# Hybrid mLSTM and stick-breaking layer on one core: each block of turned heads stored to DRAM by one transfer, regrouped by its four reads, and some of the moves at other places

## The chip, the cores and the metric

One core of a Trainium2 chip runs the whole layer in one launch. The metric is the device time of one execution in microseconds; lower is better. TensorE multiplies, VectorE (DVE), ScalarE (ACT) and GpSimd (POOL) do the rest, and SyncE (SP) issues nearly all transfers, one after the other.

## What is computed

One layer over x of 512 tokens by 1024 channels in float32, with one combined input projection whose columns feed two token mixers and the merge gates:

```python
h = rmsnorm(x, norm_w)
proj = h @ w_in + b_in
mq, mk, mv, mi, mf, mo, mz, sq, sk, sv, sz, gates = split(proj)

q, k = split(silu(causal_conv(concat(mq, mk))))          # mLSTM, 4 heads of 256
hm = mlstm_chunkwise(q, k, mv, mi, log_sigmoid(mf))
y_m = rmsnorm(hm) * sigmoid(mo) * silu(mz)

q, k = rmsnorm(sq), rmsnorm(sk)                          # stick-breaking, 8 heads of 128
z = q @ k.T * 128 ** -0.5                                # strictly causal
A[t, s] = sigmoid(z[t, s]) * prod(1 - sigmoid(z[t, j]) for s < j < t)
y_s = (A @ sv) * silu(sz)

g_m, g_s = split(sigmoid(gates))
out = x + (g_m * (y_m @ w_proj_m) + g_s * (y_s @ w_proj_s)) @ w_out
```

## The kernel before

Each float32 operand of a matmul is split into a high part (ACT copies it to float32r: `wh`) and a low part (DVE subtracts: `wl`), and a product is three matmuls (`mm3`, lines 96 to 98; line 966 in the `Half` units): high by high, high by low, low by high.

**Units.** The work of TensorE is a list of units, and the main loop (line 1500) runs over them. A unit has a weight slab of 512 KB: `load` issues it on SP into a tile `stg` (three buffers), `split` makes `wh` and `wl` (three buffers each) two units ahead, and `mm(0)` and `mm(1)` are its two halves. In the loop's body the order of the code is the order on each engine; the tables at the top of the file say in which unit the other work is written, and `defer(n, f)` writes `f` n units later. `E` is 36. The units before E are the first q group (4), four of a gate path, and two `Pair`s of 14 `Half` units of 12 matmuls each, which form products by a recursive scheme with sums of weight quarters (`X`, `Y`, `V`, `Z`) and of results (`dst`, to which GpSimd adds a tile `u` by an accumulating transfer). From E on most units have 24 matmuls. Unit E starts in the trace at 138.25 us.

**Turning q and k.** The stick-breaking heads need q and k with the channel on the partitions. For each of two sets of four heads, and for q and k, two heads (a pair g) are moved at a time:

- `turn` (in unit `TURN[name][g]`, for set 0): DVE transposes the 32x32 blocks of 256 channels by 512 tokens into a tile `ty` (line 437), four instructions.
- `move`, one unit later: SP stores `ty` to DRAM as `t_d`, four transfers of 32 partitions each (line 443).
- `back` (in unit `TZ_BACK[name, g]`, for set 0): SP reads it back, four transfers (line 450), into `tz`, where channels lie on partitions in the natural order. For q DVE then multiplies by the product of the two norm weights (line 453).
- `head(h)` starts at `SB_START`: it splits `tz` into `qtt` and `ktt` (lines 101 and 102), then scores, chains the products by a scan, and turns the result in the same way by `ay`, `a_d`, `az`.

Set 0's q is turned in units 9 and 13, so its store is long done when it is read back; its k comes out of the second `Pair` late, and is turned in units 30 and 31, with the first head starting in unit E-1. The mLSTM heads turn their output in the same way, by `ht`, `h_d` and `hz` (lines 865 to 897). The tiles `ty` of set 0, `tz`, `qtt`, `ktt`, the raw q and the `dst` pairs share nine buffers of the tag `qk`; which one a tile gets is settled when the program is built, by what is free at that place.

In units E-1 and E besides: `gates()` (line 611) runs 16 matmuls for the mLSTM gates, and ACT copies their result (line 621).

A transfer on SP also waits until the one eight places before it has landed, since eight completion semaphores are used in turn.

Of the kernel before, what the change touches and what calls it, by code (L numbers as in the profile page):

```python
# [8 lines left out]
F32 = mybir.dt.float32  # L9
# [3 lines left out]
OP = mybir.AluOpType  # L13

D = 1024
T = 512
KT = 8
TB = 4
# [10 lines left out]
E = 4 + FILL + 14 * PAIRS  # L29
SB_START = [E + n for n in (-1, 2, 5, 8, 14, 16, 18, 20)]  # L30
M_START = [E + n for n in (37, 41, 54, 60)]
GATES_PREP, GATES_START, GATES_SCAN = E - 3, E - 1, E + 26
TURN = {"q": (9, 13), "k": (30, 31)}
TZ_BACK = {("q", 0): E - 4, ("q", 1): E + 1, ("k", 0): E - 3, ("k", 1): E + 2}
REST = {E + n for n in (7, 48)}
AHEAD, LOADS = 2, 4

# [2 lines left out]
def tile_hybrid_layer(  # L40
# [16 lines left out]
    nc = tc.nc  # L57
# [3 lines left out]
    def pool(name, bufs=1, **k):  # L61
        return ctx.enter_context(tc.tile_pool(name=name, bufs=bufs, **k))
# [3 lines left out]
    sp = pool("sp")  # L66
    mp = pool("mp")
    tiny = pool("tiny", 4)
    dp = pool("dp", space=bass.MemoryType.DRAM)
# [9 lines left out]
    def blk(tag, dt=F32, shape=(512,), name=None, p=128):  # L79

        where = mp if tag in MISC else sp
        return where.tile([p] + list(shape), dt, name=name or tag, tag=tag, bufs=BUFS[tag])

    def two(tag, dt=F32, name=None):

        t = blk(tag, dt, (2, 512), name=name)
        return t[:, 0, :], t[:, 1, :]
# [12 lines left out]
    def split(src, hi, lo):  # L100
        nc.scalar.activation(hi, src, AF.Copy)  # L101
        nc.vector.tensor_tensor(lo, src, hi.bitcast(F32), op=OP.subtract)  # L102
# [96 lines left out]
    now = [0]  # L199

    def defer(n, fn):
        later.setdefault(now[0] + n, []).append(fn)
# [26 lines left out]
    qkw = cst.tile([128, 1], F32, name="qkw")  # L229
# [124 lines left out]
    class SbSet:  # L354
# [71 lines left out]
        def turns(self, name):  # L426
            for g in range(2):
                if self.s:
                    defer({"q": (1, 2), "k": (1, 2)}[name][g], lambda g=g: self.turn(name, g))
                else:  # L430
                    later.setdefault(TURN[name][g], []).append(lambda g=g: self.turn(name, g))

        def turn(self, name, g):
            ty = sp.tile([128, 8, TB, 32], F32, name="ty", tag=("qk", "A")[self.s],
                         bufs=BUFS[("qk", "A")[self.s]])
            for tb in range(TB):
                nc.vector.transpose(ty[:, :, tb, :],  # L437
                                    self.raw[name][tb][:, 256 * g:256 * g + 256].rearrange("p (x j) -> p x j", j=32))

            def move():  # L440
                park = dp.tile([32, 2, 4, 4, 128], F32, name="t_d", tag="t_d", bufs=4)
                for a in range(4):
                    nc.sync.dma_start(park[:, :, :, a].rearrange("i h b x -> i (h b) x"),  # L443
                                      ty[32 * a:32 * a + 32].rearrange("i g n j -> i g (n j)"))

                def back():
                    tz = blk("qk", F32, (2, 4, 128), name="tz")
                    self.tz[name, g] = tz
                    for b in range(4):
                        nc.sync.dma_start(tz[32 * b:32 * b + 32].rearrange("i h a x -> i h (a x)"),  # L450
                                          park[:, :, b].rearrange("i h a x -> i h (a x)"))
                    if name == "q":
                        defer(2, lambda: nc.vector.tensor_scalar(tz, tz, qkw, None, op0=OP.mult))

                if self.s:
                    defer(1, back)
                else:
                    later.setdefault(TZ_BACK[name, g], []).append(back)

            defer(1, move)  # L460
# [11 lines left out]
        def head(self, h):  # L472
            hs = slice(h * 128, (h + 1) * 128)
            tr = []
            for name in ("q", "k"):
                th, tl = own = two("qk", FR, name=name + "tt")
                tp = self.tz[name, h // 2][:, h % 2].rearrange("p a (i j) -> p i a j", j=32)
                th, tl = [x.rearrange("p (i a j) -> p i a j", a=4, j=32) for x in own]
                split(tp, th, tl)
                tr.append(own)  # L480
# [66 lines left out]
            park = dp.tile([4, 32, 4, 320], F32, name="a_d", tag="a_d", bufs=3)  # L547
# [11 lines left out]
            def turn(js):  # L559
# [5 lines left out]
                for j in js:  # L565
                    o, n = (slot[j, j] - n0) * 128, T - j * 128
                    a_parts[j] = ah[:, o:o + n], al[:, o:o + n]

            turn((0,))
            turn((1,))  # L570
            yield
            op = att_ps()
# [5 lines left out]
            apply(0)  # L578
            apply(1)
            turn((2, 3))  # L580
            yield
            apply(2)
# [117 lines left out]
    class MPair:  # L700
# [89 lines left out]
        def head(self, h):  # L790
# [48 lines left out]
            hns = blk("P5", shape=(TB, 256), name="hns")  # L839
# [22 lines left out]

            ht = sp.tile([128, 8, TB, 32], F32, name="ht", tag="A", bufs=4)

            def turn(i):
                nc.vector.transpose(ht[:, :, i, :], hns[:, i, :].rearrange("p (x j) -> p x j", j=32))

            scale = [num(0), num(1)]  # L870
            for i in (2, 3):
                yield
                for fn in scale:
                    fn()
                if i == 3:
                    turn(0)
                    turn(1)
                scale = [num(i)]
            yield
            scale[0]()  # L880
            turn(2)
            yield
            turn(3)
            yield
            hz = sp.tile([128, 2, T], F32, name="hz", tag="A", bufs=4)
            park = dp.tile([32, 2, 4, 4, 128], F32, name="h_d", tag="h_d", bufs=2)
            for b in range(4):
                nc.sync.dma_start(park[:, :, :, b].rearrange("i d a x -> i (d a) x"),
                                  ht[32 * b:32 * b + 32].rearrange("i g n j -> i g (n j)"))
            yield  # L890
            for a in range(4):
                nc.sync.dma_start(hz[32 * a:32 * a + 32], park[:, :, a].rearrange("i d b x -> i d (b x)"))
            yield
            for d in range(2):
                y = y_m[2 * hd + d].rearrange("p (i b j) -> p i b j", i=TB, b=4)
                z = hz[:, d, :].rearrange("p (b i j) -> p i b j", i=TB, b=4)
                nc.vector.tensor_tensor(y, z, y, op=OP.mult)


# [600 lines left out]
    for c in range(N):  # L1500
# [34 lines left out]
        for e in list(pend):  # L1535
            if c >= e[0] and e[2]():
                pend.remove(e)
                g = e[3]()
# [36 lines left out]
```

## Time and profile before

| | |
|---|---|
| time, median of 3 runs | 685.08 us (683.88 to 686.15) |
| the profiled execution | 685.25 us, its span 683.5 us, 9343 instructions |
| TensorE busy | 672.9 us, 98% of the span |
| DVE, ACT, POOL busy | 506.3, 366.5, 121.6 us |
| transfers | 116.70 MB, 133200 packets on SP's queue, 53.1% of 16 engines' span |

The page gives busy time by engine, the span in 40 slices, the DMA queues, the chain of work that ended last, and the costliest groups of instructions. Further views of the same trace list who waited for whom, the instructions of an engine in order of time, and the busy share, granted TensorE clock and DMA share of any stretch. Times in them are counted from the span's start. A wait in square brackets names how long the engine stood idle before an instruction and what released it. Where a row ends in x4, four instructions were merged.

### The profile page before, as it was taken

The page shows a single profiled execution, that of the slowest core. Times are in us where ns is not written, and L with a number is a line of the kernel's source. Part 1 is how long each engine was busy: PE and PEld are TensorE (multiplying, and loading weights), DVE is VectorE, ACT ScalarE, POOL GpSimd, SP SyncE. Part 2 cuts the span into 40 slices and gives each one's busy share as a digit, 9 for nine tenths or more (in the row PEclk, how much of TensorE's full clock was granted, in tenths as well). Part 3 has the DMA queues.
Part 4 walks back from the last instruction along what each step waited for, and adds up shares of the span by engine and source line. Part 5 has one row for each costly group of instructions (what it writes and reads, how often), then busy time and mean ns, then how long its engine had stood idle before and what let it go on. Part 6 is the DMA issues. An engine that isn't in the chain of part 4 may idle for free.

```text
span 683.5 us, 9343 instructions
## 1 busy us (share of the span) xinstructions
PE 672.9 (98%) x3098; PEld 560.8 (82%) x3098; DVE 506.3 (74%) x866; ACT 366.5 (54%) x696; POOL 121.6 (18%) x259
## 2 busy tenths in 40 slices
PE   8999999979999999999999999999999999999998
PEld 6888888858888888888888888888888888888876
DVE  6887988748788868978788654569973466477997
ACT  7576567244776365644654747344455854234451
POOL 4023153212545013310011101110000120001020
PEclk9999999999999999999999999999999999999999
DMA  7567785796758976737368632435344478957333
GB/s 251 144 209 191 223 210 119 165 306 209 210 158 234 270 213 194 215 117 207 93 129 184 140 107 62 133 100 153 93 139 126 124 222 258 275 183 161 116 82 103
DMA packets 137568, 116.70 MB, mean 171 GB/s; under 512 B 17658, under 2 KB 108180, under 8 KB 137520
## 3 DMA queue, kind: packets, MB, share of 16 engines
q1 hardware_dynamic: 133200, 106.02, 53.1%
q0 software_dynamic: 4176, 9.96, 8.0%
q8 instruction: 24, 0.39, 0.2%
q14 instruction: 24, 0.20, 0.1%
q10 hardware_dynamic: 144, 0.13, 0.1%
HBM read 85.10 MB, written 21.03 MB: 155 GB/s over the span
## 4 chain that ended last, share of the span: by engine, by line
PE 78%; DMA 2%; DVE 2%; SPq 1%; issue 1%; ACT 0%; ACTq 0%; DVEq 0%
PE dps L96 22%; PE dps L97 22%; PE dps L98 22%; PE aps L97 3%; PE aps L98 3%; PE aps L96 3%; DMA stg<-in_w_in_dram 1%; PE aps L848 1%; PE aps L850 1%; PE aps L849 1%; DMA dst<-u 1%; DVE wl L102 1%; SPq L450 0%; SPq L443 0%; DVE ty L437 0%
## 5 line engine op out<-in xcount | busy, mean ns | idle before, releaser
L96 PE MATMUL dps<-hh,wh 128*128 128x512 f32 x448 | 175.0, 391 | 0.0
L98 PE MATMUL dps<-hh,wl 128*128 128x512 f32 x448 | 174.6, 390 | 0.0
L97 PE MATMUL dps<-hl,wh 128*128 128x512 f32 x448 | 174.4, 389 | 0.0
L102 DVE TENSOR_TENSOR wl<-stg,wh 128x1024 fp32r<-128x1024 f32 x79 | 96.5, 1222 | 81.5 <-ACT wh L101 80.8
L101 ACT ACTIVATE wh<-stg 128x1024 fp32r<-128x1024 f32 x79 | 83.1, 1054 | 57.6 <-PE dps L97 27.4
L98 PEld LDWEIGHTS dps<-hh,wl 128*128 128x128 f32 x448 | 84.1, 188 | 17.8
L97 PEld LDWEIGHTS dps<-hl,wh 128*128 128x128 f32 x448 | 84.2, 188 | 16.7
L96 PEld LDWEIGHTS dps<-hh,wh 128*128 128x128 f32 x448 | 84.2, 188 | 16.7
L97 PE MATMUL dps<-wl,hh 128*128 128x512 f32 x96 | 37.8, 393 | 0.8 <-DVE wl L102 0.8
L738 ACT ACTIVATE tmp<-acc 128x512 f32<-128x512 f32 x16 | 10.1, 633 | 52.9 <-DVE acc L735 52.9
L96 PE MATMUL dps<-wh,hh 128*128 128x512 f32 x96 | 38.0, 396 | 0.0
L98 PE MATMUL dps<-wh,hl 128*128 128x512 f32 x96 | 37.6, 392 | 0.0
L735 DVE SCALAR_TENSOR_TENSOR acc<-tmp,vec,acc 128x511 f32<-128x511 f32 (+2 forms) x48 | 36.0, 750 | 1.7
L501 POOL TENSOR_SCALAR_AFFINE_SELECT om<-om 128x128 f32<-128x128 f32 x32 | 19.8, 617 | 90.4 <-ACT om L499 90.3
L499 ACT ACTIVATE om<-aps,rq 128x512 f32<-128x512 f32 (+3 forms) x32 | 16.8, 524 | 18.3 <-PE aps L98 18.3
L511 DVE TENSOR_TENSOR_SCAN om<-om 128x512 f32<-128x512 f32 (+3 forms) x32 | 26.2, 819 | 0.0
L96 PE MATMUL dps<-yh,wh 128*128 128x512 f32 x64 | 24.9, 389 | 0.0
L97 PE MATMUL dps<-yl,wh 128*128 128x512 f32 x64 | 24.9, 389 | 0.0
L98 PE MATMUL dps<-yh,wl 128*128 128x512 f32 x64 | 24.9, 389 | 0.0
L858 ACT ACTIVATE hns<-aps,hst 128x256 f32<-128x256 f32 x16 | 7.6, 475 | 27.8 <-DVE hst L857 20.8
L97 PEld LDWEIGHTS dps<-wl,hh 128*128 128x128 f32 x96 | 18.3, 191 | 4.5 <-DVE wl L102 1.1
L96 PEld LDWEIGHTS dps<-wh,hh 128*128 128x128 f32 x96 | 18.3, 191 | 3.7 <-ACT wh L101 0.2
(299 smaller groups left out, 1510.7 us busy)
## 6 DMA issues: line engine op xcount, KB each, us to landing
stg<-in_w_in_dram SPq DMA_DIRECT2D x71, 512.0 KB, 4.8
a_d<-ay SPq DMA_DIRECT2D x8, 640.0 KB, 2.9
az<-a_d SPq DMA_DIRECT2D x32, 160.0 KB, 5.4
t_d<-ty SPq DMA_DIRECT2D x32, 128.0 KB, 3.7
tz<-t_d SPq DMA_DIRECT2D x32, 128.0 KB, 4.5
stg<-in_w_proj_s_dram SPq DMA_DIRECT2D x8, 512.0 KB
B<-in_w_out_dram SPq DMA_DIRECT2D x8, 512.0 KB, 6.9
stg<-in_w_proj_m_dram SPq DMA_DIRECT2D x8, 512.0 KB, 3.6
```

Source lines behind the costliest of these rows:

```text
L96: nc.tensor.matmul(ps, ah, bh, start=first, stop=False)
L97: nc.tensor.matmul(ps, ah, bl, start=False, stop=False)
L98: nc.tensor.matmul(ps, al, bh, start=False, stop=last)
L101: nc.scalar.activation(hi, src, AF.Copy)
L102: nc.vector.tensor_tensor(lo, src, hi.bitcast(F32), op=OP.subtract)
L499: nc.scalar.activation(om[:, 0:n], zp, AF.Sigmoid, scale=rn[:, h:h + 1])
L501: nc.gpsimd.affine_select(out=om[:, ts], in_=om[:, ts], compare_op=OP.is_gt, fill=1.0, base=0, channel_multiplier=1, pattern=[[-1, 128]])
L511: nc.vector.tensor_tensor_scan(back, back, back, 1.0, op0=OP.mult, op1=OP.bypass)
L735: nc.vector.scalar_tensor_tensor(acc[:, j:], t[:, 0:T - j], cw(3 - j, ch), acc[:, j:], op0=OP.mult, op1=OP.add)
L738: nc.scalar.activation(t, acc, AF.Sigmoid)
L848: nc.tensor.matmul(nm[:, 0:258], ph, vh, start=j == 0, stop=False)
L858: nc.scalar.activation(hn, sum_v, AF.Square, scale=dn, accum_out=ssq)
```

## The change

The store of a turned block becomes one transfer of 128 whole rows of 4 KB, in the order in which `ty` (or `ht`) lies in memory; DVE's turns write `ty` in the order b, h, n, j, so that what one read needs from a row is one run of 256 floats. The four reads regroup: each takes a quarter of every row, 1 KB, in place of runs of 2 KB. `tz` and `hz` then hold (4, 256) per partition, and their readers address them so. The same is done for the mLSTM output. The three tables move: the second k of set 0 is turned one unit later, its first q is read back in unit E-10 instead of E-4 (with the multiplication staying in unit E-2), and its second q and k are read back one unit later.

```diff
-TURN = {"q": (9, 13), "k": (30, 31)}
-TZ_BACK = {("q", 0): E - 4, ("q", 1): E + 1, ("k", 0): E - 3, ("k", 1): E + 2}
+TURN = {"q": (9, 13), "k": (30, 32)}
+TZ_BACK = {("q", 0): E - 10, ("q", 1): E + 2, ("k", 0): E - 3, ("k", 1): E + 3}
...
-            ty = sp.tile([128, 8, TB, 32], F32, name="ty", tag=("qk", "A")[self.s],
+            ty = sp.tile([128, 4, 2, TB, 32], F32, name="ty", tag=("qk", "A")[self.s],
                          bufs=BUFS[("qk", "A")[self.s]])
             for tb in range(TB):
-                nc.vector.transpose(ty[:, :, tb, :],
-                                    self.raw[name][tb][:, 256 * g:256 * g + 256].rearrange("p (x j) -> p x j", j=32))
+                nc.vector.transpose(ty.rearrange("p b h n j -> p h b n j")[:, :, :, tb, :],
+                                    self.raw[name][tb][:, 256 * g:256 * g + 256].rearrange("p (h b j) -> p h b j", h=2, j=32))
 
             def move():
-                park = dp.tile([32, 2, 4, 4, 128], F32, name="t_d", tag="t_d", bufs=4)
-                for a in range(4):
-                    nc.sync.dma_start(park[:, :, :, a].rearrange("i h b x -> i (h b) x"),
-                                      ty[32 * a:32 * a + 32].rearrange("i g n j -> i g (n j)"))
+                park = dp.tile([128, 1024], F32, name="t_d", tag="t_d", bufs=4)
+                nc.sync.dma_start(park, ty.rearrange("p b h n j -> p (b h n j)"))
 
                 def back():
-                    tz = blk("qk", F32, (2, 4, 128), name="tz")
+                    tz = blk("qk", F32, (4, 256), name="tz")
                     self.tz[name, g] = tz
                     for b in range(4):
-                        nc.sync.dma_start(tz[32 * b:32 * b + 32].rearrange("i h a x -> i h (a x)"),
-                                          park[:, :, b].rearrange("i h a x -> i h (a x)"))
+                        nc.sync.dma_start(tz[32 * b:32 * b + 32],
+                                          park.rearrange("(a i) (b x) -> i b a x", a=4, b=4)[:, b])
                     if name == "q":
-                        defer(2, lambda: nc.vector.tensor_scalar(tz, tz, qkw, None, op0=OP.mult))
+                        defer(max(2, E - 2 - now[0]), lambda: nc.vector.tensor_scalar(tz, tz, qkw, None, op0=OP.mult))
...
-                tp = self.tz[name, h // 2][:, h % 2].rearrange("p a (i j) -> p i a j", j=32)
+                tp = self.tz[name, h // 2].rearrange("p a (h i j) -> p h i a j", h=2, j=32)[:, h % 2]
...
-            park = dp.tile([32, 2, 4, 4, 128], F32, name="h_d", tag="h_d", bufs=2)
-            for b in range(4):
-                nc.sync.dma_start(park[:, :, :, b].rearrange("i d a x -> i (d a) x"),
-                                  ht[32 * b:32 * b + 32].rearrange("i g n j -> i g (n j)"))
+            hz = sp.tile([128, 4, 256], F32, name="hz", tag="A", bufs=4)
+            park = dp.tile([128, 1024], F32, name="h_d", tag="h_d", bufs=2)
+            nc.sync.dma_start(park, ht.rearrange("p a d n j -> p (a d n j)"))
```

On SP, from the bias rows of the second `Pair` (`prow`) to the weights after unit E, the order before is this; `v_park` are stores of v, `i_d` and `f_d` those of the gates, and the three `stg` in a row are the weights of units E+1 to E+3.

```order
L1020 DMA prow<-in_b_in_dram 128x512 x2
L1055 DMA v_park<-dst 128x512 x2
L443 DMA t_d<-ty 256x1x128 x4
L450 DMA tz<-t_d 32x2x512 x4
L443 DMA t_d<-ty 256x1x128 x4
L121 DMA stg<-in_w_in_dram 128x2x512
L450 DMA tz<-t_d 32x2x512 x4
L121 DMA stg<-in_w_in_dram 128x2x512 x3
L1055 DMA v_park<-dst 128x512 x2
```

In the changed kernel (its lines there are one to two lower) the same piece of SP's queue reads:

```order
L1018 DMA prow<-in_b_in_dram 128x512 x2
L448 DMA tz<-t_d 32x4x256 x4
L1053 DMA v_park<-dst 128x512 x2
L442 DMA t_d<-ty 128x1024
L121 DMA stg<-in_w_in_dram 128x2x512
L448 DMA tz<-t_d 32x4x256 x4
L442 DMA t_d<-ty 128x1024
L121 DMA stg<-in_w_in_dram 128x2x512 x3
L1053 DMA v_park<-dst 128x512 x2
```

The first q read stands ahead of the v stores instead of between the two k stores, unit E's weights ahead of the first k read and of the second k store, and the second k store behind the first k read.

On DVE, from the first k turn to the low part of unit E-2's weights (`wl<-Z`; the `wl<-V` are those of units E-4 and E-3, `vl` is a part of v, and `dst<-prow` adds a bias), before:

```order
L437 STREAM_TRANSPOSE ty<-dst 128x8x32 x4
L102 TENSOR_TENSOR wl<-V,wh 128x1024
L466 TENSOR_TENSOR vl<-dst,vh 128x512
L437 STREAM_TRANSPOSE ty<-dst 128x8x32 x4
L102 TENSOR_TENSOR wl<-V,wh 128x1024
L1035 TENSOR_TENSOR dst<-prow,dps 128x512 x2
L102 TENSOR_TENSOR wl<-Z,wh 128x1024
```

and in the changed kernel:

```order
L437 STREAM_TRANSPOSE ty<-dst 128x2x4x32 x4
L102 TENSOR_TENSOR wl<-V,wh 128x1024
L464 TENSOR_TENSOR vl<-dst,vh 128x512
L102 TENSOR_TENSOR wl<-V,wh 128x1024
L1033 TENSOR_TENSOR dst<-prow,dps 128x512 x2
L437 STREAM_TRANSPOSE ty<-dst 128x2x4x32 x4
L102 TENSOR_TENSOR wl<-Z,wh 128x1024
```

The second k turn moves behind unit E-3's low part and the two bias adds.

More of the change, by code (lines that the diff above doesn't have):

```diff
@@ L861, in num @@
                 return lambda: nc.scalar.activation(hn, sum_v, AF.Copy, scale=r)
-            ht = sp.tile([128, 8, TB, 32], F32, name="ht", tag="A", bufs=4)
+            ht = sp.tile([128, 4, 2, TB, 32], F32, name="ht", tag="A", bufs=4)
             def turn(i):
-                nc.vector.transpose(ht[:, :, i, :], hns[:, i, :].rearrange("p (x j) -> p x j", j=32))
+                nc.vector.transpose(ht.rearrange("p a d n j -> p d a n j")[:, :, :, i, :],
+                                    hns[:, i, :].rearrange("p (d a j) -> p d a j", d=2, j=32))
             scale = [num(0), num(1)]
@@ L884, in head @@
             yield
-            hz = sp.tile([128, 2, T], F32, name="hz", tag="A", bufs=4)
-            park = dp.tile([32, 2, 4, 4, 128], F32, name="h_d", tag="h_d", bufs=2)
-            for b in range(4):
-                nc.sync.dma_start(park[:, :, :, b].rearrange("i d a x -> i (d a) x"),
-                                  ht[32 * b:32 * b + 32].rearrange("i g n j -> i g (n j)"))
+            hz = sp.tile([128, 4, 256], F32, name="hz", tag="A", bufs=4)
+            park = dp.tile([128, 1024], F32, name="h_d", tag="h_d", bufs=2)
+            nc.sync.dma_start(park, ht.rearrange("p a d n j -> p (a d n j)"))
             yield
             for a in range(4):
-                nc.sync.dma_start(hz[32 * a:32 * a + 32], park[:, :, a].rearrange("i d b x -> i d (b x)"))
+                nc.sync.dma_start(hz[32 * a:32 * a + 32],
+                                  park.rearrange("(b i) (a x) -> i a b x", a=4, b=4)[:, a])
             yield
@@ L895, in head @@
                 y = y_m[2 * hd + d].rearrange("p (i b j) -> p i b j", i=TB, b=4)
-                z = hz[:, d, :].rearrange("p (b i j) -> p i b j", i=TB, b=4)
+                z = hz.rearrange("p b (d i j) -> p d i b j", d=2, j=32)[:, d]
                 nc.vector.tensor_tensor(y, z, y, op=OP.mult)
```

## Prediction

> **What bounds the kernel now.** I read the page's busy shares first, then TensorE's waits, then TensorE's own rows around the longest wait, and last the chain of waits and the rows of SP's queue that lead up to it.
>
> ```profile
> PE 672.9 (98%) x3098; PEld 560.8 (82%) x3098; DVE 506.3 (74%) x866; ACT 366.5 (54%) x696; POOL 121.6 (18%) x259
> ```
>
> TensorE is the bound: a transfer or a vector instruction is worth nothing unless TensorE waits for it. In TensorE's list of waits three entries lie in the body of the kernel; the rest are at its start.
>
> ```profile
> PE aps L96 <- ACT ktt L101: 2.4, 1, 2.4
> ...
> PE aps L97 <- DVE ktt L102: 0.9, 1, 0.9
> PE dps L97 <- DVE wl L102: 0.8, 1, 0.8
> ```
>
> All three stand within 10 us, at unit E and the scores of the first stick-breaking head. TensorE's rows there (start, duration), and below them the same nine score matmuls (three each of 512, 128 and 256 columns) in a later head, undisturbed:
>
> ```profile
> 138.25 0.46 PE L96 MATMUL dps<-wh,hh 128*128 128x512 f32 x1
> ...
> 140.04 0.39 PE L96 MATMUL dps<-wh,hh 128*128 128x512 f32 x1
> ...
> 141.85 0.39 PE L98 MATMUL dps<-wh,hl 128*128 128x512 f32 x1
> 144.67 0.49 PE L96 MATMUL aps<-ktt,qtt 128*128 128x512 f32 x1 [2.43 <-ACT ktt L101]
> 146.10 0.54 PE L97 MATMUL aps<-ktt,qtt 128*128 128x512 f32 x1 [0.93 <-DVE ktt L102]
> 148.14 0.63 PE L96 MATMUL dps<-wh,hh 128*128 128x512 f32 x1
> 149.84 0.40 PE L97 MATMUL dps<-wl,hh 128*128 128x512 f32 x1
> ...
> 165.85 0.39 PE L96 MATMUL aps<-ktt,qtt 128*128 128x512 f32 x1
> 167.22 0.40 PE L96 MATMUL dps<-wh,hh 128*128 128x512 f32 x1
> ```
>
> From 140.04 to 141.85 eight 512-column matmuls start in 1.81 us, 0.227 each. After 148.14 four take 1.70 us: TensorE runs there at half clock. In stretches of the trace (PE busy, ..., granted clock, DMA share, GB/s) one sees both that and the state of the DMA engines:
>
> ```profile
> 116.00:120.00 4.00, 4.00 (x18) 3.02 (x17) 3.97 (x5) 3.89 (x7) 0.00 (x0) 1.00 0.01 2
> 128.00:132.00 4.00, 4.00 (x19) 3.30 (x19) 2.40 (x8) 0.00 (x0) 1.58 (x2) 1.00 1.03 204
> 140.00:144.00 4.00, 2.24 (x10) 1.50 (x9) 0.45 (x2) 1.48 (x2) 0.00 (x0) 1.00 1.03 390
> 147.00:149.00 2.00, 2.00 (x10) 1.81 (x9) 1.37 (x2) 1.89 (x4) 1.14 (x4) 0.50 1.05 315
> ```
>
> The DMA engines are idle at 116 to 120 and full from 128 on; full means 204 GB/s where the transposed blocks with their 512-byte pieces are stored, and 390 where weights in 2 KB rows come in. The chain of waits says what the scores waited for:
>
> ```profile
> 130.46 1.29 SPq L121
> ...
> 131.80 1.19 SPq L450
> ...
> 135.37 7.07 DMA stg<-in_w_in_dram
> ...
> 142.52 1.06 ACT wh L101
> ...
> 145.44 0.61 DVE ktt L102
> ```
>
> ScalarE splits the weights of unit E+1 before the head's q and k, in order; those weights were issued only at 135.37 and took 7.07 us. They were late because SP stood in four groups of small transfers:
>
> ```profile
> 121.64 2.53 SPq L443 DMA_DIRECT2D t_d<-ty  x4
> 124.21 2.54 SPq L450 DMA_DIRECT2D tz<-t_d  x4
> 126.84 3.52 SPq L443 DMA_DIRECT2D t_d<-ty  x4
> 130.46 1.29 SPq L121 DMA_DIRECT2D stg<-in_w_in_dram  x1
> 131.80 3.47 SPq L450 DMA_DIRECT2D tz<-t_d  x4
> ```
>
> These are the first k store, the first q read, the second k store, the weights of unit E, the first k read.
>
> **What the stall costs.** Three pieces, each against the undisturbed rows. Start of unit E: 138.25 to 140.04 is 1.79 us for three matmuls, which take 0.68: 1.11. First scores: 141.85 + 0.23 = 142.08 to 148.14 is 6.06 us against 167.22 - 165.85 = 1.37: 4.69. The four slow matmuls: 1.70 against 0.91: 0.79. Together 6.59 us. No other wait of TensorE after 20 us is in its list, so that is all that the change can win; units after E follow one another without a gap and shift as a whole.
>
> **The change part by part.** Rows for its prices (DMA issues with KB each and median us to landing; three rows of SP; two of VectorE; the last gate matmul and the copy of its result; the last score part of the first head; ScalarE's split for head 2):
>
> ```profile
> a_d<-ay SPq DMA_DIRECT2D x8, 640.0 KB, 2.9
> az<-a_d SPq DMA_DIRECT2D x32, 160.0 KB, 5.4
> t_d<-ty SPq DMA_DIRECT2D x32, 128.0 KB, 3.7
> tz<-t_d SPq DMA_DIRECT2D x32, 128.0 KB, 4.5
> ...
> 164.14 0.34 SPq L548 DMA_DIRECT2D a_d<-ay  x1
> 98.23 0.82 SPq L1020 DMA_DIRECT2D prow<-in_b_in_dram  x2
> 113.08 1.76 SPq L1055 DMA_DIRECT2D v_park<-dst  x2
> 123.24 1.41 DVE L437 STREAM_TRANSPOSE ty<-dst 128x256 f32<-128x256 f32 x4
> 126.88 1.21 DVE L102 TENSOR_TENSOR wl<-Z,wh 128x1024 fp32r<-128x1024 f32 x1
> 135.30 0.39 PE L619 MATMUL aps<-hl,wg 128*128 128x512 f32 x1
> 138.18 0.59 ACT L621 ACTIVATE g<-aps 36x512 f32<-36x512 f32 x1
> 154.41 0.33 PE L96 MATMUL aps<-ktt,qtt 128*128 128x384 f32 x1
> 177.13 0.62 ACT L101 ACTIVATE qtt<-tz 128x512 fp32r<-128x512 f32 x1
> ```
>
> Stores: 12 moves (8 of q and k, 4 of the mLSTM output) lose three of their four issues, 36 in all. Near the stall that is six, and the two stores fall from 2.53 and 3.52 us of SP to one issue each; the kernel has such a store already (whole rows, 640 KB): 0.34 us, landing after 2.9. I take 0.4 and 2.9; the upper ends are 0.88 (the dearest quarter of a group above) and 3.7.
>
> Transfer time of a store: at 204 GB/s 512 KB take 2.6 us, at 390 1.3. I take 1.3, since whole rows are nearer to the weights' 2 KB rows; keep 2.6. [...]
>
> Reads: still four, in 1 KB pieces instead of 2 KB. Nearest row: 160 KB in pieces of 1,280 bytes land in 5.4 us, which per byte is 4.3 for 128 KB against 4.5 now. I cost it at nothing; the upper end is the stores' rate, one more us per group of 512 KB.
>
> First q read: goes to unit E-10, behind the two bias rows that SP issued at 98.23 to 99.05, hence at 99 to 101.7. SP's next work there are the v stores at 113, so nothing is delayed; the multiplication by the norm weights stays at unit E-2. It takes 2.54 us of SP and 1.3 to 2.6 us of transfer out of the full stretch.
>
> Second k: turned one unit later. On VectorE its 1.41 us now stand behind the unit's two bias adds instead of ahead of a weight split, so the low half of unit E-2's weights (126.88 to 128.09) has the same work ahead of it as before. The turns write another order of the same 32x32 blocks; I cost that at nothing (source, sizes and runs of 32 stay); if each doubled from 0.35, the first k turn and its store would come 1.4 us later, and TensorE could wait about that once.
>
> Second q and k reads: one unit later. The second k tile now falls into the buffer of the first head's k operand, so SP waits for that head's last scores (154.41 before, 148 when shifted), and the weight loads behind it wait too. Reads from 148 land by 155; the second q and k are split for head 2 at 177.13, 170 when shifted. Hidden, with 15 us to spare.
>
> The new course of SP: first k store 121.6 to 122.0; weights of unit E 122.4 (was 130.46); the first k reads wait for the store's landing, 124.5 to 125.3, and take 2.5 to 3.5, to 127.0 to 128.8; second k store to 129.2 at most; weights of E+1 once the split at 126.88 is done (128.1), so 128.1 to 129.6 instead of 135.37. Deadline: TensorE is ready for the scores at 138.25 + 12 x 0.227 = 140.97; before, its second score matmul stood 146.10 - 142.44 = 3.66 us behind the landing, and without the wait would start at 141.2, so the weights must land by 137.5. With 7.07 us, the worst, they land at 136.7 at the latest; with half of that at 133. What is late next is not a transfer: the copy of the gates on ScalarE stands ahead of that split and waits for the gate matmuls, which end about 135.7. Copy 0.6, to 136.4, then the 3.58 us from 142.52 to 146.10: 140.0, against 141.2. It holds by 1.2 us.
>
> Sum: all 6.59 us go. The profiled execution took 685.25 us (span 683.5 and 1.75 around it); less 6.59 it is 678.66. The median of the runs is 0.17 lower; I say **678.6**.
>
> **Rivals.**
> *A rest of the wait.* The margin of 1.2 us is eaten by ScalarE or VectorE, and TensorE waits 1 to 2 us at the scores. For it: both engines work in order there. Against: from 128 to 132 ScalarE shows 0.00 of 4 us busy and VectorE 2.40. The clock fell after 2.43 and 0.93 us of idling with one matmul between; the 0.8 us at the start of unit E had not lowered it. So a rest costs itself alone: about 680.0. [...]
>
> *The transfers are the bound, not SP's queue*, so that the change does not do what it says. For it: DMA share 1.03 from 128 on. If stores and reads keep their time and only the first q group's 1.3 us (512 KB at 390 GB/s) leave, the weights of E+1 land at 141.1, and the scores still wait; 1.11 + 1.3 are won: 682.8. Against: the engines stand idle just before (0.01), which now takes the first k store and unit E's weights.
>
> *SP's head blocked by the store it reads back (slower).* Between the first k store and its reads there was the q group; now SP waits at the reads until the store has landed, with all weight loads behind. If landing takes L, the weights of E+1 go out at 121.6 + L + 4, worse than 135.37 from L = 10; at L = 12 about 2 us are lost: 687. Against: whole rows land in 2.9 us.
>
> **How the numbers follow.** All of the stall gone: 0.75 (677.5 to 679.7, as the three runs before lie up to 1.2 us from their median). A rest: 0.11. Transfers the bound: 0.08. Slower: 0.03. The remaining 0.03 is a gain beyond the sum. The range 677.3 to 681.3 holds the first two and part of the rest. 0.3% is 2.1 us, about what a measurement here can tell from no change: faster needs below 683.0, which the first two cases, the last, and half of the third give: 0.93; same 0.04; slower 0.03.
>
> **What would show it.** Right: no wait of TensorE on ktt or wl between 120 and 160, granted clock 1.00 throughout, weights of unit E issued near 122 and of E+1 near 129, DMA share under 0.9 around 130, TensorE's last matmul 6 to 7 us earlier. A rest shows as one wait on ktt at full clock; bound transfers as a share near 1 with a landing over 7 us; the blocked head as a long SP wait on the store at the k reads. Wrong it would be, too, if a wait appears later, at head 2 or at the tail, where none stands now.

## The result, and the profile after

The changed kernel takes 677.57 us (median of 4 runs), against 685.51 for the kernel before on the same chip: ratio 0.9888, interval 0.9869 to 0.9907. Its profiled execution took 677.94 us with a span of 676.2, before 685.25 and 683.5. In a later comparison, on another chip, it was 677.61 against 684.74 (ratio 0.990, 0.988 to 0.9919). One execution of the run `f3` below (837.26 us) and one of `g3` (2533.77 us) had a far lower granted clock (0.75 and 0.26) and are left out of the ratios; without its one, `f3`'s median is 683.62 instead of 683.75.

The busy shares and, under them, TensorE's whole list of waits in the changed kernel (us in total, times, longest):

```profile
PE 668.7 (99%) x3098; PEld 558.1 (83%) x3098; DVE 506.7 (75%) x866; ACT 366.9 (54%) x696; POOL 119.3 (18%) x259
...
PE dps L1414 <- DVE idle L1409: 1.5, 1, 1.5
PE aps L309 <- DVE x L301: 1.4, 2, 0.7
PE dps L1446 <- DVE hh L313: 1.0, 1, 1.0
```

The three waits at unit E and the first head have gone; what is left stands at the kernel's start. TensorE's rows there (first matmul of unit E, first two score matmuls, first matmul behind the scores):

```profile
137.24 0.39 PE L96 MATMUL dps<-wh,hh 128*128 128x512 f32 x1
...
139.96 0.39 PE L96 MATMUL aps<-ktt,qtt 128*128 128x512 f32 x1
140.18 0.39 PE L97 MATMUL aps<-ktt,qtt 128*128 128x512 f32 x1
...
141.32 0.40 PE L96 MATMUL dps<-wh,hh 128*128 128x512 f32 x1
```

From unit E's start to the matmul behind the scores it is 4.08 us, before 9.89 (138.25 to 148.14). That is 5.81, and with the 0.79 of the four slow matmuls behind 6.60.

SP's queue in the changed kernel, on the way to the weights of unit E+1 (the last row):

```profile
98.09 3.69 SPq L448 DMA_DIRECT2D tz<-t_d  x4
...
120.65 0.32 SPq L442 DMA_DIRECT2D t_d<-ty  x1
121.06 0.39 SPq L121 DMA_DIRECT2D stg<-in_w_in_dram  x1
123.53 1.74 SPq L448 DMA_DIRECT2D tz<-t_d  x4
126.02 0.34 SPq L442 DMA_DIRECT2D t_d<-ty  x1
127.13 0.40 SPq L121 DMA_DIRECT2D stg<-in_w_in_dram  x1
```

Those weights go out at 127.13 instead of 135.37. ScalarE's and VectorE's rows from the copy of the gates on:

```profile
134.72 0.60 ACT L619 ACTIVATE g<-aps 36x512 f32<-36x512 f32 x1 [5.28 <-PE aps L617]
135.21 1.05 ACT L101 ACTIVATE wh<-stg 128x1024 fp32r<-128x1024 f32 x1
136.17 0.62 ACT L101 ACTIVATE qtt<-tz 128x512 fp32r<-128x512 f32 x1
136.69 0.62 ACT L101 ACTIVATE ktt<-tz 128x512 fp32r<-128x512 f32 x1
...
138.04 0.68 DVE L102 TENSOR_TENSOR ktt<-tz,ktt 128x512 fp32r<-128x512 f32 x1
```

The split of the weights (`wh`) begins at 135.21 behind the gates, with no wait of its own: they had landed by then, at most 8.1 us after their issue. The trace also keeps sixteen marks of landing for each such transfer, as its parts arrive: for these weights the first stands at 132.64 and the last, which is the landing, at 133.73, 6.6 us after the issue. k's low part ends at 138.72; TensorE needs it at 140.18: a slack of 1.46 us.

### The profile page after: what moved, and what is told of

It is laid out like the page before. It is cut to its first block, busy times and chain, and to the rows that moved or that the text cites. A ratio compares the mean times of both kernels' runs of the same rounds, so it can differ in the third digit from the quotient of the medians.

```text
span 676.2 us, 9297 instructions
## 1 busy us (share of the span) xinstructions
PE 668.7 (99%) x3098; PEld 558.1 (83%) x3098; DVE 506.7 (75%) x866; ACT 366.9 (54%) x696; POOL 119.3 (18%) x259
## 4 chain that ended last, share of the span: by engine, by line
PE 97%; DMA 1%; POOL 1%; SPq 0%; DVE 0%; ACT 0%; issue 0%
PE dps L96 24%; PE dps L97 24%; PE dps L98 24%; PE dps L964 6%; PE aps L964 5%; PE aps L97 3%; PE aps L98 3%; PE aps L96 3%; PE dps L1446 1%; PE dps L1448 1%; PE dps L1447 1%; DMA stg<-in_w_in_dram 1%; PE aps L846 1%; PE aps L848 1%; PE aps L847 1%; PE aps L309 0%
## 5 line engine op out<-in xcount | busy, mean ns | idle before, releaser
L499 POOL TENSOR_SCALAR_AFFINE_SELECT om<-om 128x128 f32<-128x128 f32 x32 | 17.1, 536 | 86.3 <-ACT om L497 86.3
L98 PEld LDWEIGHTS dps<-wh,hl 128*128 128x128 f32 x96 | 18.0, 188 | 3.8
```

The costliest lines, as they stand in the source:

```text
L98: nc.tensor.matmul(ps, al, bh, start=False, stop=last)
L499: nc.gpsimd.affine_select(out=om[:, ts], in_=om[:, ts], compare_op=OP.is_gt, fill=1.0, base=0, channel_multiplier=1, pattern=[[-1, 128]])
```

## The experiments

For each run the text on record is followed by what it measured. "Landed" is read from the start of the split of unit E+1's weights, where ScalarE's row names that transfer as what ended its wait; it agrees with the last mark of landing to 0.1 us.

**The tables alone, in the old layout** (`e1`): the old stores and reads; the three tables and the multiplication's place as changed.

```diff
-TURN = {"q": (9, 13), "k": (30, 31)}
+TURN = {"q": (9, 13), "k": (30, 32)}
-TZ_BACK = {("q", 0): E - 4, ("q", 1): E + 1, ("k", 0): E - 3, ("k", 1): E + 2}
+TZ_BACK = {("q", 0): E - 10, ("q", 1): E + 2, ("k", 0): E - 3, ("k", 1): E + 3}
```

> The three tables of the change with the old layout: four stores per block in 512-byte runs. Theory (SP's queue): the first q read is out of the way, but the four stores and the wait for their landing stand ahead of the first k read, and the second k store's four issues ahead of the weights of unit E+1, which go out at about 134 instead of 135.4 and 128. The wait at the start of unit E goes (1.1 us), most of the wait at the scores stays: 680 to 683.5 us. Rival (the transfers are the bound): 1.3 us less of transfer ahead of these weights, 682.8. If the change is mainly its places: 677.6.

683.04 us (ratio 0.9958, 0.9939 to 0.9978); its seven executions run from 679.16 to 685.81, and the profiled one is the slowest. SP's second k store and the weights of E+1, the split of these, and TensorE's two waits:

```profile
131.17 2.59 SPq L443 DMA_DIRECT2D t_d<-ty  x4
...
142.11 1.06 ACT L101 ACTIVATE wh<-stg 128x1024 fp32r<-128x1024 f32 x1 [4.87 <-DMA stg<-in_w_in_dram]
...
PE aps L96 <- ACT ktt L101: 2.2, 1, 2.2
...
PE aps L97 <- DVE ktt L102: 0.7, 1, 0.7
```

Here the later second k turn, with four slow transfers per store, holds SP until 133.76, and the weights behind it land at 142.07. Issued so late they can hardly be in time, though the first q has left the queue: by the prediction's reckoning they are needed 0.75 us ahead of unit E, which is 138.4 here (unit E starts at 139.16), 4.5 us after the issue, and the shortest landing of these weights given here is 6.1 us (`e3`).

**The layout alone, with the old tables** (`e2`): the changed kernel with the two table lines of before.

> The new layout (one store of whole rows, reads in 1 KB pieces) with the old tables, first q read between the two k stores. Theory (SP's queue): stores take 0.4 us of SP instead of 2.5 and 3.5, the q read fills the time in which the first k store lands, weights of unit E at about 125.5 and of E+1 at about 128.5: no wait left, 677.6 to 678.6 us, as with the whole change. Rival (transfers): only the stores' 2.6 us leave, q's read stays in the stretch, weights of E+1 land near 139.8, and 681 to 682 are left.

678.76 us (0.9916, 0.9886 to 0.9945), little more than the changed kernel takes. Its four executions run from 677.15 to 682.13, and the profiled one (span 680.4) is the slowest. In its chain of waits stands

```profile
127.39 11.57 DMA stg<-in_w_in_dram
```

so in this execution the weights of E+1 are issued 8 us earlier than before and land only 3.5 earlier. SP was no longer the obstacle; the transfers were. TensorE's waits there, and one of its stretches of 1 us behind them (the granted clock is the number ahead of DMA share and GB/s):

```profile
PE aps L97 <- DVE ktt L102: 0.9, 1, 0.9
PE aps L96 <- ACT ktt L101: 0.8, 1, 0.8
...
144.00:145.00 1.00, 1.00 (x5) 1.00 (x6) 0.90 (x1) 0.98 (x3) 0.53 (x1) 0.50 1.02 354
```

Two short waits, and the clock is at half. At 677.15 us and a mean granted clock of 1.00 another execution can have had neither, so these waits differ from one execution to the next.

**The early read of the first q alone** (`e3`, and again as `g4`): the kernel before with one number changed.

```diff
-TZ_BACK = {("q", 0): E - 4, ("q", 1): E + 1, ("k", 0): E - 3, ("k", 1): E + 2}
+TZ_BACK = {("q", 0): E - 10, ("q", 1): E + 1, ("k", 0): E - 3, ("k", 1): E + 2}
...
-                        defer(2, lambda: nc.vector.tensor_scalar(tz, tz, qkw, None, op0=OP.mult))
+                        defer(max(2, E - 2 - now[0]), lambda: nc.vector.tensor_scalar(tz, tz, qkw, None, op0=OP.mult))
```

> Before, with the first q read alone moved to unit E-10; old layout, k as before. Theory (SP's queue): eight store issues, then weights of unit E at about 128, the first k read to 131, weights of E+1 at about 131.5, landing 135 to 138.5 against a deadline of 137.5: nothing or a short rest of the wait is left, 678 to 680.5 us. Rival (transfers): 1.3 us less in the stretch, 682.8.

678.59 us (0.9908, 0.9893 to 0.9923), with no wait at the scores. The weights of E+1 and their split:

```profile
129.65 4.18 SPq L121 DMA_DIRECT2D stg<-in_w_in_dram  x3
...
135.81 1.06 ACT L101 ACTIVATE wh<-stg 128x1024 fp32r<-128x1024 f32 x1 [0.80 <-DVE g L623]
```

They went out 5.7 us earlier than before, in the old layout, and landed 6.1 us after that (last mark 135.73); the split waited for something else.

**Four stores of whole rows** (`e4`): the changed kernel, each block of q and k stored by four transfers of 32 whole rows.

```diff
-                nc.sync.dma_start(park, ty.rearrange("p b h n j -> p (b h n j)"))
+                for a in range(4):
+                    nc.sync.dma_start(park[32 * a:32 * a + 32],
+                                      ty[32 * a:32 * a + 32].rearrange("p b h n j -> p (b h n j)"))
```

> The whole change, but each block stored by four transfers of 32 whole rows in place of one of 128: same pieces and bytes, three more issues per store. Theory (SP's queue): weights of unit E+1 go out 2 to 4 us later than with one store (at 130 to 132) and land at 134 to 139 against 137.5: 677.6 to 680 us, and SP's rows show the store four times as long. Rival (transfers): nothing changes, 677.6, with the weights issued as with one store.

678.90 us (0.9907, 0.9892 to 0.9922), no wait at the scores. A store takes 1.7 to 2.6 us of SP instead of 0.3, the weights go out at 130.03, and it still holds.

**A short and a longer wait at the scores** (`f1`, `f2`): the changed kernel with extra high copies of the first head's q on ScalarE, 6 and 12 of them.

```diff
+                for _ in range(6 if name == "q" and h == 0 and self.s == 0 else 0):
+                    nc.scalar.activation(th, tp, AF.Copy)
                 split(tp, th, tl)
```

> The changed kernel, with the high copy of the first head's q written seven times instead of once on ScalarE (the six extra ones give the same values), nothing else. Each takes 0.52 us from start to start; the low part of k ends 1.46 us before TensorE needs it in the changed kernel, so six make the second score matmul wait about 1.2 to 1.7 us, in one or two pieces. The question is the price of such a short wait. Theory A (the prediction's 'a rest costs itself alone'): the granted clock stays 1.00 behind it, and the time is 677.6 + 1.2 to 1.7, about 679. Theory B (a short wait also halves the clock for a stretch, as 1.73 us did in the kernel with the new layout and the old places): the time is about 680 to 681, and the matmuls behind the scores start 0.45 instead of 0.23 us apart for 3 to 4 us.

681.31 us (0.9934, 0.9915 to 0.9953). The extra copies took 0.66 us each, not 0.52. TensorE's waits, and behind them its stretches of 1 us (PE, PEld, DVE, ACT, POOL busy, granted clock, DMA share, GB/s):

```profile
PE aps L96 <- ACT ktt L101: 1.2, 1, 1.2
...
PE aps L97 <- DVE ktt L102: 0.3, 1, 0.3
...
142.00:143.00 1.00, 0.92 (x4) 0.76 (x5) 1.00 (x3) 0.20 (x2) 0.00 (x0) 0.78 0.00 0
143.00:144.00 1.00, 1.00 (x6) 1.00 (x6) 1.00 (x2) 1.00 (x2) 0.27 (x1) 0.50 0.00 0
144.00:145.00 1.00, 1.00 (x4) 0.81 (x4) 0.36 (x1) 0.86 (x3) 1.00 (x4) 0.50 0.00 0
145.00:146.00 1.00, 1.00 (x4) 0.81 (x3) 0.00 (x0) 0.00 (x0) 0.33 (x3) 0.51 0.49 70
146.00:147.00 1.00, 1.00 (x6) 0.79 (x5) 0.00 (x0) 0.00 (x0) 0.00 (x0) 1.00 0.83 289
```

0.78 over 1 us is 0.44 us at half clock, then 1, 1 and 0.98: 3.42 us, which cost half of that, 1.71. With the 1.53 us of waiting it is 3.24 of the 3.7 us by which this kernel is slower than the changed one. Theory B holds here: 1.53 us of idling was enough. Five of the six executions lie at 681.12 to 682.22; the sixth took 679.89 with a mean granted clock of 1.00 and seems to have paid the wait alone.

> The changed kernel, with the high copy of the first head's q written thirteen times instead of once on ScalarE. Twelve extra copies are 6.2 us: the scores should wait about 4.3 us in all, less than the 6.6 us stall of the kernel before but more than any rest. If the slow clock behind a wait is a fixed stretch (3 to 7 us at half, so 1.5 to 3.5 us lost), the time is 677.6 + 4.3 + 1.5 to 3.5, 683.4 to 685.4; if the wait costs itself alone, 681.9.

686.47 us (1.001, 0.9996 to 1.0025): as slow as the kernel before. The wait was 5.18 us:

```profile
PE aps L96 <- ACT ktt L101: 5.2, 1, 5.2
...
143.00:144.00 1.00, 0.00 (x0) 0.00 (x0) 0.00 (x0) 0.96 (x2) 0.00 (x0) 0.96 0.00 0
...
150.00:151.00 1.00, 1.00 (x4) 0.77 (x4) 0.00 (x0) 0.00 (x0) 0.00 (x0) 0.63 1.02 389
```

The clock was at half from 143.92 to 150.74 (0.50 in the six rows between): 6.82 us, against 3.42 in `f1`. 5.87 of it lay behind the wait, which ended at 144.87, and cost 2.94; with the wait 8.1, of 8.9 measured. More than was expected, because the copies were longer; the slow stretch, with its 6.82 us, lies within the 3 to 7 us that were expected.

**All of the change but the early read** (`f3`): the changed kernel with one number put back.

```diff
-TZ_BACK = {("q", 0): E - 10, ("q", 1): E + 2, ("k", 0): E - 3, ("k", 1): E + 3}
+TZ_BACK = {("q", 0): E - 4, ("q", 1): E + 2, ("k", 0): E - 3, ("k", 1): E + 3}
```

> The changed kernel, with its first q read back in unit E-4 as before, behind the first k store; all else (layout, k turn one unit later, second reads one unit later) as changed. The early q read alone gave nearly the whole gain; this asks whether it is needed. If SP's queue is what counts, it moves the weights of unit E+1 from 127.1 to about 129.5, inside the 131 or so that a landing of 6 us allows, and the time stays at 677.5 to 678.5 with no wait at the scores. If the transfers count as well (in the kernel with the new layout and the old places those weights took 11.6 us to land), they land near 139, the scores wait 1 to 2 us, and the time is 678.5 to 680.5.

683.75 us (0.9971, 0.9954 to 0.9988): nearly all of the gain is lost, more than either theory said. SP's q read-back and the weights of E+1, the split of these, and TensorE's two waits:

```profile
120.75 2.18 SPq L448 DMA_DIRECT2D tz<-t_d  x4
...
126.86 0.40 SPq L121 DMA_DIRECT2D stg<-in_w_in_dram  x1
...
140.50 1.06 ACT L101 ACTIVATE wh<-stg 128x1024 fp32r<-128x1024 f32 x1 [5.45 <-DMA stg<-in_w_in_dram]
...
PE aps L96 <- ACT ktt L101: 2.8, 1, 2.8
...
PE aps L97 <- DVE ktt L102: 0.9, 1, 0.9
```

The weights are issued 0.27 us *earlier* than in the changed kernel and land at 140.46, 13.6 us after the issue and 6.7 us later than there. Their sixteen marks of landing lie far apart: eleven by 136.39, the other five from 138.96 to 140.41. TensorE waits 2.80 and 0.92 us and then runs 3.42 us at half clock (the rows of 1 us from 143 on show 0.97, 0.50, 0.50, 0.50 and 0.82), half of which is lost: 3.72 + 1.71 = 5.4 us, nearly the whole difference of the spans (681.8 - 676.2 = 5.6).

Side by side, the parts of the change do not add up:

| first q read in | layout | second k turn, second reads | us |
|---|---|---|---|
| E-4 | old | as before | 685.51 (before) |
| E-10 | old | as before | 678.59 (`e3`), 677.98 (`g4`) |
| E-4 | new | as before | 678.76 (`e2`) |
| E-10 | old | one unit later | 683.04 (`e1`) |
| E-4 | new | one unit later | 683.75 (`f3`) |
| E-10 | new | one unit later | 677.57 (changed) |

The early read and the new layout each bring nearly the whole gain by itself. The second k turn and the second reads one unit later cost 4.5 us beside the early read alone (`e1` against `e3`), 4 to 5 us beside the layout alone (`f3` against `e2`, on two chips), and little beside both, where the kernel is the fastest of all (that pair without them was not run). With them the second k store goes out right ahead of the weights of E+1 (125.75 in `f3`, 123.95 in `e2`); whether that is why was not tested.

**SP's time, bytes, or the reads themselves** (`g1`, `g2`, `h1`): the changed kernel with extra transfers behind the first k store, where `f3` has its q read-back. `g1`: six of 4 KB. `g2`: one of 512 KB in 2 KB pieces, DRAM to DRAM. `h1`: the four reads of the parked q once more, into DRAM. `g3` is the changed kernel itself beside `g1`, `g2` and `g4`.

```diff
+                if not self.s and (name, g) == ("k", 0):      # g1
+                    for i in range(6):
+                        nc.sync.dma_start(dp.tile([128, 8], F32, name="xtra%d" % i), w_in[0:128, 0:8])
...
+                    nc.sync.dma_start(dp.tile([256, 512], F32, name="xtra"), w_in[0:256, 0:512])      # g2
...
+                    for b in range(4):      # h1: self.pq is the parked block of the first q
+                        nc.sync.dma_start(xtra[32 * b:32 * b + 32],
+                                          self.pq.rearrange("(a i) (b x) -> i b a x", a=4, b=4)[:, b])
```

> The changed kernel with six extra transfers of 4 KB each (128 pieces of 32 bytes, weights to an unused place in DRAM) behind the first k store: some 2 us of SP's time and almost no bytes, at the place of the four q reads of the kernel that keeps the early read out (683.75 us). Theory SP (the prediction's: what made the weights late is the time SP stood in its queue): the weights of unit E go out 2 us later, those behind them are pushed likewise, and the scores wait, so 679 to 683.5. Theory DMA (the bytes moved between 120 and 140 us make them late, whoever issues them): nothing changes, 677 to 678.5, no wait at the scores.

> The changed kernel with one extra transfer of 512 KB (2 KB pieces, weights to an unused place in DRAM) at that same place: one issue of about 0.4 us of SP, and as many bytes as a q read-back. Theory SP: nothing changes, 677 to 678.5. Theory DMA: the weights of unit E+1, issued as early as in the changed kernel, land 2 to 5 us later; they had landed by 135.2 us at the latest, and 137.5 is needed, so the scores wait 0 to 3 us and the time is 679 to 683.5.

> The changed kernel as it is, beside the next one on the same chip: 677.6 us, no wait at the scores.

> The kernel before with the early read of the first q alone, again (678.59 us in another comparison). If the rest of the change is worth nothing, it is within 0.5 us of the changed kernel here. If the late landing that its trace showed (weights of unit E+1 split at 140.07) leaves it at the edge, some of its executions wait at the scores and pay the slow clock, and its median is 1 to 2 us above.

> The changed kernel, whose first q is still read early, with the same four reads once more behind the first k store, into an unused place in DRAM instead of SBUF: the same 1 KB pieces of the same rows, at the place where they cost 6 us when they brought the q itself (683.75). An extra 512 KB in one transfer of 2 KB pieces cost nothing there (677.73), nor did six extra issues (677.89). If it is the regrouping reads as such (four issues, 512 pieces of 1 KB, gathered out of every row of the parked block), the weights of unit E+1 land near 140 again and the time is 681 to 684. If it is what the reads write to (32 partitions of SBUF, in a buffer that others wait for), nothing changes: 677 to 678.5.

| | us | ratio to before | issue to landing of E+1's weights |
|---|---|---|---|
| `g1` | 677.89 | 0.9899 (0.9881 to 0.9916) | 127.83 to 135.42 |
| `g2` | 677.73 | 0.9897 (0.988 to 0.9914) | 127.04 to 135.14 at the latest |
| `g3` | 677.61 | 0.990 (0.988 to 0.9919) | 126.77 to 134.87 at the latest |
| `g4` | 677.98 | 0.990 (0.9883 to 0.9918) | 129.84 to 136.44 |
| `h1` | 681.59 | 0.996 (0.9937 to 0.9983) | 129.20 to 139.99 |

The rows behind that: `g1`'s extra issues and its split; `g4`'s split; `h1`'s extra reads, its split and TensorE's two waits:

```profile
120.50 3.84 SPq L445 DMA_DIRECT2D xtra<-in_w_in_dram  x6
...
135.46 1.06 ACT L101 ACTIVATE wh<-stg 128x1024 fp32r<-128x1024 f32 x1 [0.66 <-DMA stg<-in_w_in_dram]
```

```profile
136.48 1.06 ACT L101 ACTIVATE wh<-stg 128x1024 fp32r<-128x1024 f32 x1 [1.32 <-DMA stg<-in_w_in_dram]
```

```profile
122.81 2.57 SPq L448 DMA_DIRECT2D xtra<-t_d  x4
...
140.03 1.06 ACT L101 ACTIVATE wh<-stg 128x1024 fp32r<-128x1024 f32 x1 [2.92 <-DMA stg<-in_w_in_dram]
...
PE aps L97 <- DVE ktt L102: 0.9, 1, 0.9
PE aps L96 <- ACT ktt L101: 0.3, 1, 0.3
...
145.00:146.00 1.00, 1.00 (x6) 0.81 (x5) 0.88 (x1) 1.00 (x4) 0.86 (x1) 1.00 0.52 201
```

`g1`'s 3.84 us of SP's time cost nothing, but mostly because SP would have waited at that place (2.0 us for the store's landing alone): the weights of E+1 went out only 0.70 us later than in the changed kernel, so `g1` does not try a late issue of them. With `g2`'s 512 KB in 2 KB pieces ahead of them they landed at 134.20 by the last mark, 7.2 us after the issue, in time. Behind the four regrouping reads, 512 pieces of 1 KB, they took 13.6 us (`f3`, into SBUF) and 10.8 us (`h1`, into DRAM): where the reads write is not the cause. The size of the pieces, the block that is read and its gathering were not tried apart. Small pieces as such explain little: between 118 and 144 us in `f3` a packet of 1 KB on SP's queue took 46 ns at the median and one of 2 KB 84, a tenth more per byte.

`h1` waited 1.2 us in this execution and kept its full clock there. Of the 3.3 us by which its span is longer than the changed kernel's, 1.8 lie ahead of unit E, which starts at 139.03 instead of 137.24; its ten executions run from 678.24 to 685.53.

The expectation of `g4` rests on a misread row: in `e3`'s trace the split at 140.07 is that of unit E+2's weights. `g4` and `g3` differ by 0.37 us: beside the early read the rest of the change is worth no more than that here, and some slack (the weights' last mark is at 136.39 in `g4`, 133.07 in `g3`).

What the four reads cost the stretch from 120 to 140 us, in the changed kernel, in `f3` and in `g2`:

```profile
120.00:140.00 20.00, 20.00 (x90) 16.56 (x89) 16.44 (x28) 7.92 (x9) 4.87 (x6) 1.00 0.94 272
...
120.00:140.00 20.00, 19.85 (x88) 16.12 (x86) 12.54 (x22) 4.79 (x5) 4.87 (x6) 1.00 0.96 264
...
120.00:140.00 20.00, 20.00 (x90) 16.57 (x89) 16.43 (x28) 7.90 (x9) 4.87 (x6) 1.00 0.99 293
```

`f3` and `g2` have the same 512 KB more to move; `g2` moved 293 x 20 = 5.86 MB and `f3` 5.28, at about the same share. 0.58 MB at 264 GB/s is 2.2 us, an estimate of what the engines lost with the reads in the stream. The order shows more. In `f3` six groups of 512 KB and the four 256 KB of `u` stand up to and including E+1's weights, 4.19 MB, but by 140 us 5.28 had moved. Later transfers overtook part of these weights: the first mark of E+2's stands at 135.16, ahead of the last five of E+1's. From their issue to the first mark the weights of E+1 took 5.5 us in the changed kernel, 6.8 in `f3`, 6.9 in `h1` and 7.8 in `e2`; from the first mark to the last 1.1 us, and then 6.8, 3.8 and 3.7. So most of the delay is that a few parts of one transfer lag behind the others. Which DMA engines they belong to the trace does not keep, and why they lag is open.

## Why the prediction was right, and where it was not

- **The size.** The stall was put at 1.11 + 4.69 + 0.79 = 6.59 us; 6.60 went. The forecast was 678.6 (its own terms, 685.25 - 6.59 - 0.17, give 678.5), the median is 1.0 lower. The two spans differ by 7.3, and 1.0 of it lies ahead of anything changed: unit E is reached at 137.24 instead of 138.25. The first 20 us, before and after:

```profile
0.00:20.00 20.00, 16.80 (x62) 12.84 (x63) 13.65 (x32) 14.12 (x32) 7.12 (x19) 0.91 0.69 228
...
0.00:20.00 20.00, 16.04 (x69) 12.17 (x70) 13.76 (x32) 14.21 (x33) 7.33 (x19) 1.00 0.68 228
```

  The execution that the sum was made against had a slow stretch at its start, (1 - 0.91) x 2 x 20 = 3.6 us; the one after had none. About 0.3 is given back behind unit E.
- **The course of SP** came as written: weights of unit E at 121.06 (122.4 forecast), k reads at 123.53 to 125.27 (124.5 to 128.8), second k store at 126.02 (129.2 at most), weights of E+1 at 127.13 (128.1 to 129.6). The first store landed within the 2.88 us from its issue to the first read (2.9 forecast), and the reads did not block SP: the slower rival did not come.
- **What is late next** was right: the copy of the gates, with 1.46 us of slack (1.2 forecast).
- **The cause was only half right.** "They were late because SP stood in four groups of small transfers" fits the kernel before and `e1`: weights issued at 135.37 or 133.86 can hardly be in time when the shortest landing of these weights given here is 6.1 us (`e3`), and issued at 129.65 to 130.03 (`e3`, `g4`, `e4`) they were. What the issue alone would be worth in the kernel before stays open, for the first mark of its weights (140.97) comes right behind the last of the k reads ahead of them (140.94). The steps that failed are "with 7.07 us, the worst", and the reads in 1 KB pieces "at nothing; the upper end ... one more us per group of 512 KB": with q's reads among the transfers the weights went out at 126.86 to 129.20 and took 13.6 us (`f3`), 11.6 (`e2`, in its slowest execution) and 10.8 (`h1`). The changed kernel escapes this because its q is read at E-10, which was moved for 2.54 us of SP and 1.3 to 2.6 us of transfer. That the total came out is in part luck: one part of the change hid what another would have cost.
- **The rival "the transfers are the bound"** had the mechanism of `f3` and `h1`, but also sized the q group at 1.3 us, and so wrongly said that the scores would still wait.
- **The DMA share** was forecast under 0.9 around 130. It stayed over 1 there:

```profile
128.00:132.00 4.00, 4.00 (x19) 3.33 (x18) 4.00 (x6) 1.06 (x1) 1.92 (x3) 1.00 1.05 276
```

  But at 276 GB/s instead of 204: the engines are as busy (1.05 against 1.03) and move more.
- **"A rest costs itself alone"** was wrong. 1.53 us of idling halved the clock for 3.42 us (`f1`), so that a rest of the wait would have given about 682, not 680.0. `e2`'s profiled execution did the same after 0.8 and 0.9, for 3.40 us (0.93, 0.50, 0.50, 0.50 and 0.87 in the rows of 1 us from 142 on), while after 1.2 in `h1` the clock stayed at 1.00. How much idling brings the slow stretch is not shown.
- **Layout, turns and the second k** were costed at nothing. For DVE's turns that holds: four took 1.42 us, before 1.41 to 1.42. The layout was worth nearly the whole gain alone (`e2`), though its reads are what failed above. The later second k turn and second reads cost 4 to 5 us in `e1` and `f3`; in the whole change they leave no wait.

## What to carry to other kernels

When a load is late, look at both ends of it: the issue (is the queue's engine stuck?) and the time from issue to landing; in one execution of `e2` moving the issue 8 us forward was worth 3.5. Take a read that can be done earlier out of the stretch in which weights must land, to one where the DMA engines are less full (share 0.57 from 98 to 102 us in the kernel before, 1.03 from 128 to 132); that alone was worth nearly all 7 us here, by one number in a table. Try the parts of a change in pairs as well as alone: two of these each brought nearly everything, and the third cost 4 to 5 us beside either. And price a wait of TensorE with the slow stretch that can follow it: in `f1` 1.53 us of waiting came with 3.42 us at half clock, and the kernel was 3.7 us slower.

## What the runs showed of the hardware that was not expected

- The stretch at half clock was 3.40 us long in `e2`, 3.42 in `f1` and `f3`, and 6.82 in `f2`. It came after 1.53 us of idling in `f1` but not after 1.2 in `h1`; one execution of `f1` shows a mean clock of 1.00, so the wait alone does not settle it.
- Behind 512 KB read in 1 KB quarters of parked rows the weights took 10.8 (`h1`) and 13.6 us (`f3`) to land; behind 512 KB in 2 KB pieces at the same place 7.2 (`g2`), and 6.6 with neither.
- A transfer can land after ones issued behind it, and its parts can land far apart: over 6.8 us for the weights in `f3`, 1.1 in the changed kernel.
